# FoX attention in a hybrid trunk: diagonal probabilities masked on GpSimd, other places in SyncE's order for some transfers, query loads issued earlier

## The chip, the cores and the metric

The kernel runs on one core of one Trainium2 chip. The metric is the device time of one execution in microseconds (us), taken several times; the median is compared.

## The reference, cut to what matters

The program is one inference step of a trunk of two layers. Each layer projects the stream `x` and mixes it by three groups of heads: RWKV-7 (A), forgetting attention, called FoX (B), and gated DeltaNet (C). A gate multiplies each result, and one output projection and a LayerNorm follow. A prompt of 2048 frames and 8 running streams of 16 frames, with 1024 cached rows each, go through together. The change lies around B:

```python
def fox_attend(q, cq, qpos, k, v, ck, kpos):
    f32 = jnp.float32
    s = jnp.einsum('bqhd,bkhd->bhqk', q.astype(f32), k.astype(f32)) * (HEAD_DIM ** -0.5)
    s = s + jnp.transpose(cq, (0, 2, 1))[..., :, None] - jnp.transpose(ck, (0, 2, 1))[..., None, :]
    s = jnp.where(kpos[None, :] <= qpos[:, None], s, -jnp.inf)
    p = jax.nn.softmax(s, axis=-1)
    return jnp.einsum('bhqk,bkhd->bqhd', p, v.astype(f32))
```

`c` is the running sum of the log forget values; there are 8 heads of 64. Causality is the `where`: a key later than the query counts nothing.

## The kernel before, in words

**Stages.** Each layer goes through a projection stage, a FoX stage and an output projection. In the projection stage `proj` takes the tokens in three parts and multiplies them with groups of weight columns (`load_w` loads a raw weight `wr` and splits it into a high part `wh` and a low part `wl`; the low part is written to `wd` at its first use and loaded as `wl<-wd` later). Matmuls named `pm` and `pv` are these. Keys and queries are split into `khi` and `klo` and written to the scratch tensors KS and QS (`qs<-khi` in the profile), and the gates' inputs to PZ. The tasks of RWKV and DeltaNet run beside it, and reach into the FoX stage.

**FoX for the prompt** (`fox_prompt`). The heads go in 4 pairs, the queries in 4 blocks of 512. For a head and block `fx_max` makes scores with queries on the partitions (`mx`), and VectorE takes their row maxima (`m`); `fx_shift` turns these to two rows (`rr`, transposed by TensorE as `rrp`) and writes them into the query tile `QA`. `fx_exp` then makes the scores with 128 keys on the partitions and up to 512 queries (`st`): one matmul of `KB` and `QB`, one of `KA` and `QA` (which carry high parts, running sums and maxima), ScalarE's exponential gives `pt`. The sum of `pt` over keys (`acc`) is kept by VectorE where the key step j is a multiple of 3, and by GpSimd otherwise. `fx_pv` multiplies `pt` with the values (`fo`), two key steps of two heads at a time; these four tiles are called a **quad** here. `fx_out` divides and gates.

**The diagonal.** In the last four key steps of a block (j from 4b on) the first 128 columns of the tile hold the diagonal, and keys later than the query must go. `fx_exp` adds a third matmul there, of the constants `ngb` and `idb`, that adds a large negative number to them (`st<-idb,ngb`); `fx_max` does the same on `mx`. Per layer 4 pairs, 4 blocks, 4 steps and 2 heads make 128 of each.

**What sets the order.** A class `Model` keeps a modelled time for each tile, bank and engine while the program is written out. Every instruction goes through `Eng.__getattr__` (L246) or `PE.add` (L224; transposes, L227), so these are the lines of nearly all rows. The modelled time becomes its priority; for SyncE, whose transfers must keep one order, `Eng.order` puts each transfer by its modelled time among the ones before it, and this is fixed. `fx_pv` of a quad is put off until the modelled time at which its `pt` are ready (`self.pvt`), and other matmuls may be placed ahead of it. Transfers are issued from SyncE's queue in that order, so a transfer that waits for its data holds up all behind it.

**Opening FoX** (`open_fx`). Tiles `QA` and `KA` number 6 each; two of each exist before the stage. The other four of each are filled with constants on GpSimd (`fx_fill`), then loads of the `QA` for block 1 are issued (`fx_qa`). The cached streams (`fox_sample`) load `qx`, `kx`, `lf`, `kc` and `vc` in the same stretch. The weights of the output projection come in by `wor` near the end of the stage.

Of the kernel before, what the change touches and what calls it, by code (L numbers as in the profile page):

```python
# [14 lines left out]
TS = 16  # L15
# [89 lines left out]
class Model:  # L105
# [60 lines left out]
    def op(self, eng, kind, outs, ins):  # L166
# [13 lines left out]
        if eng == "sync":  # L180
            n = max(n * a.shape[0] for a in outs)
            cost = max(0.5, n * 4 / 3.6e5)
            end = self.place(eng, t, cost) + 2.0
            t = end - 2.0 - cost
        elif eng == "scalar" and kind == "dma_start":
            end = self.place(eng, t + 0.1, 0.45) + 2.0
            t = end - 2.45
        else:
            cost = self.cost(eng, kind, n, outs, ins)
            end = self.place(eng, t, cost)  # L190
            t = end - cost
# [107 lines left out]
class Trunk:  # L299
# [127 lines left out]
    def load_w(self, pool, key, src, kk, n, eng):  # L427
# [8 lines left out]
        if key in self.wd:  # L436
            nc.sync.dma_start(wl.bitcast(F32), self.wd[key])
        else:
            eng.tensor_tensor(wl, raw, wh.bitcast(F32), op=ALU.subtract)
            self.wd[key] = self.dram.tile([128, kk, n], F32, name="wd_" + "_".join(map(str, key)))  # L440
            nc.sync.dma_start(self.wd[key], wl.bitcast(F32))
        return wh, wl
# [93 lines left out]
    def proj(self, l, ti, groups, nxt=None):  # L536
# [91 lines left out]
        for nm, c0, S, X in (("k", 1664, self.KS[l], self.KX[l]), ("q", 1152, self.QS[l], self.QX[l])):  # L628
            if nm not in groups:
                continue  # L630
            for r in range(0, 512, 128):
# [8 lines left out]
                nc.vector.tensor_tensor(lo[:, ns:n], st[:, ns:n], hi[:, ns:n].bitcast(F32), op=ALU.subtract)  # L640
                nc.sync.dma_start(S[0, r:r + 128, tp], hi[:, ns:n].bitcast(F32))
                nc.sync.dma_start(S[1, r:r + 128, tp], lo[:, ns:n].bitcast(F32))
                if ns:
# [33 lines left out]
    def logf(self, l, ti, fs):  # L677
# [10 lines left out]
        nc.vector.scalar_tensor_tensor(out=lt, in0=f, scalar=0.0, in1=ab, op0=ALU.min, op1=ALU.subtract)  # L688
        nc.sync.dma_start(self.o["fox_logf_p"][l, 0, tp].rearrange("(j p) h -> p j h", p=128), lt[:, ns // 128:])
        if ns:  # L690
            nc.sync.dma_start(self.o["fox_logf_s"][l].rearrange("s t h -> (s t) h"), lt[:, 0])
        nc.vector.tensor_scalar(f, lt, -1.0, None, op0=ALU.mult)
        nc.sync.dma_start(self.SM[l][t0:t0 + n].rearrange("(j p) c -> p j c", p=128), fs[:, :, 8:16])
        yield
# [7 lines left out]
        if ns:  # L702
            nc.sync.dma_start(self.LX[l].rearrange("s h t -> h s t"), fr[0:8, 0:ns].rearrange("h (s t) -> h s t", t=TS))
        cr = pool.tile([8, 768], F32, tag="st", name="cr", bufs=2)
# [5 lines left out]
        self.split(ch[:, ns:n], cl[:, ns:n], cr[:, ns:n], "vector")  # L710
        nc.sync.dma_start(self.CK[l][0, :, tp], ch[:, ns:n].bitcast(F32))
        nc.sync.dma_start(self.CK[l][1, :, tp], cl[:, ns:n].bitcast(F32))

# [577 lines left out]
    def both_chain(self, x):  # L1291
# [66 lines left out]
        if x["t0"] + W == NTOK:  # L1358
            dst = self.o["gdn_wkv_p"][x["l"]].rearrange("s (p h) k v -> s p (h k) v", h=2)
            for p in range(2):  # L1360
                nc.sync.dma_start(dst[0, p], self.Sg[:, p])

# [95 lines left out]
    def gdn_chain(self, x):  # L1458
# [50 lines left out]
        for p in range(2):  # L1509
            nc.sync.dma_start(dst[:, p].rearrange("s k v -> k s v"), SS[:, :, p])  # L1510
# [39 lines left out]
    def fx_fill(self, eng, KA, QA):  # L1550
        for t in QA + KA:
            eng.memset(t[64:96].bitcast(F32), 0.0)
# [16 lines left out]
    def open_fx(self, l):  # L1569
# [98 lines left out]
    def fx_exp(self, l, pair, b):  # L1668
# [3 lines left out]
        for j in range(nk):  # L1672
# [4 lines left out]
            for hh in range(2):  # L1677
# [115 lines left out]
    def fox_sample(self, l):  # L1793
# [30 lines left out]
        for j0 in (0, 4):  # L1824
# [84 lines left out]
        z = pool.tile([128, 4, 128], F32, tag="vn", name="sfz", bufs=2)  # L1909
        nc.sync.dma_start(z, self.PZ[l][256:768, 0:SMP].rearrange("(c p) t -> p c t", p=128))  # L1910
# [4 lines left out]
        nc.sync.dma_start(self.OD[l][256:768, 0:SMP].rearrange("(c p) t -> p c t", p=128), oT)  # L1915
        self.close(pool)
# [154 lines left out]
```

## Time and profile before

| | |
|---|---|
| median of 3 runs | 4135.79 us (4131.1 to 4138.03) |
| the profiled execution, its own time | 4139.12 us |
| its span | 4137.2 us |
| mean granted TensorE clock, share of full speed | 0.95 |

The span is what the profiler saw between the first and the last instruction; the time has 1.9 us more around it. In rows, a group of instructions has its busy time, which for TensorE holds overlapped work, and the idle time of its engine just before, put down to what ended it. L224 and L246 are the lines of the helpers through which everything is issued, so groups are told apart by the names of their tiles.

### The profile page before, as it was taken

To read this page: it belongs to the slowest core of one execution; us is meant where nothing else is said; L and a number is where in the kernel's file an instruction comes from. 1 tells how busy PE (TensorE), PEld (TensorE's weight loads), DVE (VectorE), ACT (ScalarE), POOL (GpSimd) and SP (SyncE) were. 2 spreads that over 40 slices of the span, in tenths; PEclk is the share of its full clock that TensorE was granted. 3 is DMA by queue.
4 is the path that set the end of the run, shared out by engine and by line. 5 is a ranking of instruction groups with operands and counts; after the bars stand their busy time and mean duration, and the time that the engine had idled before them with its cause. 6 is when DMAs were issued, how large, how long until landed. Compare 5 with 4: busy or idle time off the path is not lost.

```text
span 4137.2 us, 78111 instructions
## 1 busy us (share of the span) xinstructions
PE 3776.2 (91%) x30554; PEld 3107.2 (75%) x30554; DVE 2700.3 (65%) x6029; ACT 1637.1 (40%) x3351; POOL 1223.7 (30%) x1073
## 2 busy tenths in 40 slices
PE   6989998999998799889999898989999888998998
PEld 6988887888887456557888888878888775665577
DVE  6475668677774677774523757577667767777645
ACT  2343434344442344542124434244435424444411
POOL 4311232122212344454222112312122124444522
PEclk9999999999998899999999999999999989999999
DMA  7744545444555677443456445554445555774332
GB/s 262 238 154 129 155 141 173 123 139 127 173 156 138 187 192 195 138 102 111 135 157 192 134 133 151 168 153 127 141 128 186 154 131 164 199 195 124 105 115 102
DMA packets 601754, 633.80 MB, mean 153 GB/s; under 512 B 153625, under 2 KB 457483, under 8 KB 601387
## 3 DMA queue, kind: packets, MB, share of 16 engines
q1 hardware_dynamic: 535228, 543.89, 45.1%
q10 hardware_dynamic: 63406, 76.01, 5.2%
q0 software_dynamic: 2752, 8.92, 0.6%
q8 instruction: 241, 3.95, 0.4%
q14 instruction: 127, 1.03, 0.1%
HBM read 437.59 MB, written 191.10 MB: 152 GB/s over the span
## 4 chain that ended last, share of the span: by engine, by line
PE 54%; DVE 19%; issue 10%; DMA 8%; POOL 4%; ACT 3%; SPq 1%; ACTq 0%; POOLq 0%; DVEq 0%
PE pm L224 21%; PE op L224 6%; PE st L224 5%; PE fo L224 4%; PE mx L224 3%; DVE itmp L246 2%; PE pv L224 2%; DVE Wi L246 2%; PE cr L224 2%; DVE y L246 2%; PE co L224 2%; DMA pc<-pc 2%; DVE xs L246 1%; DVE m L246 1%; PE cg L224 1%
## 5 line engine op out<-in xcount | busy, mean ns | idle before, releaser
L224 PE MATMUL pm<-xh,wh 128*128 128x384 f32 (+1 forms) x2784 | 987.1, 355 | 4.8 <-ACT wh L246 4.8
L224 PE MATMUL pm<-xh,wl 128*128 128x384 f32 (+1 forms) x2784 | 924.5, 332 | 23.4 <-DMA wl<-wd 14.1
L224 PE MATMUL pm<-xl,wh 128*128 128x384 f32 (+1 forms) x2784 | 923.3, 332 | 0.0
L224 PEld LDWEIGHTS pm<-xh,wh 128*128 128x128 f32 x2784 | 533.4, 192 | 43.9 <-issue 17.0
L224 PEld LDWEIGHTS pm<-xh,wl 128*128 128x128 f32 x2784 | 532.6, 191 | 27.1 <-DMA wl<-wd 16.5
L224 PEld LDWEIGHTS pm<-xl,wh 128*128 128x128 f32 x2784 | 534.0, 192 | 10.2 <-issue 9.8
L246 POOL TENSOR_TENSOR acc<-acc,pt 128x512 f32<-128x512 f32 (+2 forms) x336 | 378.3, 1142 | 347.0 <-ACT pt L246 314.0
L246 DVE TENSOR_REDUCE m<-mx 128x1 f32<-128x512 f32 (+3 forms) x640 | 371.4, 605 | 160.4 <-PE mx L224 151.6
L246 ACT ACTIVATE pt<-st 128x512 f32<-128x512 f32 (+3 forms) x640 | 330.9, 533 | 341.8 <-PE st L224 319.7
L246 ACT CAST wh<-wr 128x1024 fp32r<-128x1024 f32 (+1 forms) x198 | 207.3, 1049 | 316.8 <-PE pm L224 237.3
L224 PE MATMUL mx<-KA,QA 66*128 66x512 f32 (+3 forms) x640 | 265.1, 437 | 40.0 <-DMA QA<-qs 26.0
L224 PE MATMUL st<-QB,KB 128*128 128x512 f32 (+3 forms) x640 | 266.7, 417 | 32.1 <-DMA QB<-qs 10.7
L224 PE MATMUL fo<-pt,V 128*64 128x512 f32 (+3 forms) x1280 | 286.8, 570 | 1.1 <-ACT pt L246 1.1
L246 ACT COPY st<-pm 128x384 f32<-128x384 f32 (+1 forms) x348 | 159.2, 457 | 279.7 <-PE pm L224 265.0
L224 PE MATMUL st<-QA,KA 104*128 104x512 f32 (+3 forms) x640 | 244.0, 381 | 0.2
L246 POOL TENSOR_SCALAR SD<-Sr,dl 128x64 f32<-128x64 f32 x128 | 66.9, 537 | 594.5 <-DVE Sr L246 517.9
L224 PEld LDWEIGHTS mx<-KA,QA 66*128 66x128 f32 x640 | 128.8, 206 | 113.3 <-issue 47.0
L224 PE MATMUL op<-woh,oh 128*128 128x512 f32 x544 | 213.0, 392 | 0.7 <-ACT acc L246 0.7
L224 PE MATMUL op<-wol,oh 128*128 128x512 f32 x544 | 212.5, 391 | 0.0
L224 PE MATMUL op<-woh,ol 128*128 128x512 f32 x544 | 212.4, 390 | 0.0
L246 POOL TENSOR_TENSOR wl<-wr,wh 128x1024 fp32r<-128x1024 f32 x58 | 142.1, 2451 | 191.9 <-ACT wh L246 171.6
L246 DVE TENSOR_TENSOR itmp<-N,Wi 128x126 f32<-128x126 f32 (+22 forms) x558 | 178.7, 320 | 15.1
(378 smaller groups left out, 7616.8 us busy)
## 6 DMA issues: line engine op xcount, KB each, us to landing
wr<-in_w_in SPq DMA_DIRECT2D x198, 512.0 KB
wl<-wd SPq DMA_DIRECT2D x116, 512.0 KB
kc<-in_cache_fox_k SPq DMA_DIRECT2D x32, 1024.0 KB
vc<-in_cache_fox_v SPq DMA_DIRECT2D x32, 1024.0 KB
wd<-wl SPq DMA_DIRECT2D x58, 512.0 KB
xin<-xd SPq DMA_DIRECT2D x78, 256.0 KB
y<-xd SPq DMA_DIRECT2D x34, 512.0 KB
ol<-od SPq DMA_DIRECT2D x34, 512.0 KB
```

Source lines behind the costliest of these rows:

```text
L224: self.add(lambda: self.eng.matmul(out, a, b, start=start, stop=stop), out, a, b, cyc, start)
L246: r = f(*a, **b)
```

## The change

1. `fx_exp` no longer adds the mask matmul to `st` on the diagonal. After the exponential GpSimd sets the entries of `pt[:, :128]` to zero whose key is later than the query (`affine_select`, which goes by position and reads no mask). The mask matmul on `mx` stays.
2. A class `Lag` issues some transfers with 6 us added to their modelled time, so they take a later place in SyncE's order. These are write-outs (`wd`, `qs<-khi` and `klo`, log forget values, running sums, states, `od<-oT`) and loads of the gates' inputs `z` and of everything that `fox_sample` reads. The model now also knows that a load from a scratch tensor (name beginning with SC) comes after the write to it.
3. `open_fx` issues the loads of `QA` for block 1 ahead of the fills, and fills `QA[2:4]` first, then `KA[2:]` and `QA[4:]`.

```diff
+        self.lag = 0.0
...
             if a.space == bass.MemoryType.DRAM:
                 dram = True
+                if a.tensor.name.startswith("SC"):
+                    t = max(t, self.done.get(a.tensor.name, 0.0) - self.lag)
...
-            end = self.place(eng, t, cost) + 2.0
+            end = self.place(eng, t + self.lag, cost) + 2.0
...
+class Lag:
+    BY = 6.0
...
+    def dma_start(self, *a):
+        self.m.lag = self.BY
+        r = self.eng.dma_start(*a)
+        self.m.lag = 0.0
+        return r
...
-            nc.sync.dma_start(self.wd[key], wl.bitcast(F32))
+            nc.lag.dma_start(self.wd[key], wl.bitcast(F32))
...
-                nc.sync.dma_start(S[0, r:r + 128, tp], hi[:, ns:n].bitcast(F32))
-                nc.sync.dma_start(S[1, r:r + 128, tp], lo[:, ns:n].bitcast(F32))
+                nc.lag.dma_start(S[0, r:r + 128, tp], hi[:, ns:n].bitcast(F32))
+                nc.lag.dma_start(S[1, r:r + 128, tp], lo[:, ns:n].bitcast(F32))
...
-        nc.sync.dma_start(z, self.PZ[x["l"]][r0:r0 + 256, x["t0"]:x["t0"] + W].rearrange("(q p) t -> p q t", p=128))
+        nc.lag.dma_start(z, self.PZ[x["l"]][r0:r0 + 256, x["t0"]:x["t0"] + W].rearrange("(q p) t -> p q t", p=128))
...
-        self.fx_fill(nc.gpsimd, self.KA[2:], self.QA[2:])
         self.fx_qa(l, 0, 1)
+        self.fx_fill(nc.gpsimd, (), self.QA[2:4])
+        self.fx_fill(nc.gpsimd, self.KA[2:], self.QA[4:])
...
-                self.pe.matmul(p[:, :w], ka[0:104, ks], qa[0:104, q0:], start=False, stop=not diag)
-                if diag:
-                    self.pe.matmul(p[:, :128], self.ngb, self.idb, start=False, stop=True)
+                self.pe.matmul(p[:, :w], ka[0:104, ks], qa[0:104, q0:], start=False, stop=True)
                 pt = pool.tile([128, 512], F32, tag="pt", name="pt", bufs=8)
                 nc.scalar.activation(pt[:, :w], p[:, :w], AF.Exp, scale=0.125)
+                if diag:
+                    nc.gpsimd.affine_select(out=pt[:, :128], in_=pt[:, :128], pattern=[[1, 128]], compare_op=ALU.is_ge, fill=0.0, base=0, channel_multiplier=-1)
...
-        nc.sync.dma_start(qx, self.QX[l].rearrange("(c p) t -> p c t", p=128))
+        nc.lag.dma_start(qx, self.QX[l].rearrange("(c p) t -> p c t", p=128))
...
-                nc.sync.dma_start(t, i["cache_fox_" + nm[0]][l, s, hf * 512:hf * 512 + 512].rearrange("(j p) h d -> p j (h d)", p=128))
+                nc.lag.dma_start(t, i["cache_fox_" + nm[0]][l, s, hf * 512:hf * 512 + 512].rearrange("(j p) h d -> p j (h d)", p=128))
```

The class adds two lines, so the helpers' lines become L227, L230 and L249. What it does to the order of instructions shows at three places.

First place: TensorE in layer 1, pair 2, block 3, around the `fo` matmuls of its first diagonal quad (`st` are the scores, `idb` and `ngb` the mask). Before:

```order
L224 MATMUL st_41000<-QA5_36152,KA5_36156 128x384
L224 MATMUL st_41000<-idb_87,ngb_88 128x128
L224 MATMUL st_41007<-QB_40037,KB_39509 128x256
L224 MATMUL st_41007<-QA4_36151,KA4_36155 128x256
L224 MATMUL st_41007<-idb_87,ngb_88 128x128
L224 MATMUL st_41016<-QB_40040,KB_39514 128x256
L224 MATMUL st_41016<-QA5_36152,KA5_36156 128x256
L224 MATMUL st_41016<-idb_87,ngb_88 128x128
L224 MATMUL fo_40559<-pt_40963,V_39512 64x512
L224 MATMUL fo_40559<-pt_40978,V_39517 64x512
L224 MATMUL fo_40559<-pt_40988,V_39512 64x384
L224 MATMUL fo_40559<-pt_41004,V_39517 64x384
```

and with the change, the same quad, one row further at each end:

```order
L227 MATMUL st_41000<-QB_40040,KB_39508 128x384
L227 MATMUL st_41000<-QA5_36275,KA5_36279 128x384
L227 MATMUL st_41007<-QB_40037,KB_39503 128x256
L227 MATMUL st_41007<-QA4_36274,KA4_36278 128x256
L227 MATMUL st_41016<-QB_40040,KB_39508 128x256
L227 MATMUL st_41016<-QA5_36275,KA5_36279 128x256
L227 MATMUL fo_40616<-pt_40962,V_39506 64x512
L227 MATMUL fo_40616<-pt_40977,V_39511 64x512
L227 MATMUL fo_40616<-pt_40987,V_39506 64x384
L227 MATMUL fo_40616<-pt_41003,V_39511 64x384
L227 MATMUL st_41027<-QB_40037,KB_39503 128x128
```

The three mask matmuls are gone, and nothing has come between the last scores and `fo`. On POOL (GpSimd) the selects of this quad's four `pt` now stand so, with the adds of the sums `acc` between:

```order
L249 AFFINE_SELECT pt_40962<-pt_40962 128x128
L249 AFFINE_SELECT pt_40977<-pt_40977 128x128
L249 AFFINE_SELECT pt_40987<-pt_40987 128x128
L249 TENSOR_TENSOR acc_40505<-acc_40505,pt_40987 128x384
L249 AFFINE_SELECT pt_41003<-pt_41003 128x128
L249 TENSOR_TENSOR acc_40506<-acc_40506,pt_41003 128x384
```

The select of the fourth `pt` (`pt_41003`) has come to stand behind an add.

Second place: SyncE's transfers as FoX opens in layer 0, behind the last weight loads `wl` (`QA2` and `QA3` are the query tiles for block 1). Before:

```order
L246 DMA wl_14779<-wd_0_3080_5575 128x1024
L246 DMA z_15026<-pz0_108 128x2x256
L246 DMA out_gdn_wkv_p<-Sg_14846 128x64 x2
L246 DMA QB_14940<-qs0_114 64x512
L246 DMA QB_14943<-qs0_114 64x512
L246 DMA KB_14946<-ks0_112 64x1024
L246 DMA V_14949<-vs0_124 128x8x64
L246 DMA QB_14940<-qs0_114 64x512
L246 DMA QB_14943<-qs0_114 64x512
L246 DMA KB_14946<-ks0_112 64x1024
L246 DMA KB_14951<-ks0_112 64x1024
L246 DMA QA2_14914<-qs0_114 64x512
```

and with the change:

```order
L249 DMA wl_14735<-wd_0_3080_5575 128x1024
L249 DMA QA2_14845<-qs0_114 64x512
L249 DMA QA3_14846<-qs0_114 64x512
L249 DMA QB_14871<-qs0_114 64x512
L249 DMA QB_14874<-qs0_114 64x512
L249 DMA KB_14877<-ks0_112 64x1024
L249 DMA V_14880<-vs0_124 128x8x64
L249 DMA QB_14871<-qs0_114 64x512
L249 DMA QB_14874<-qs0_114 64x512
L249 DMA KB_14877<-ks0_112 64x1024
```

`QA2` and `QA3` have moved ahead of all `QB`, `KB` and `V`, and the gate's `z` and the state's write-out `out_gdn_wkv_p` have moved behind.

Third place: the same queue, some transfers later (`QB_15161` before and `QB_15108` after are the queries for block 1; `qx`, `kx`, `lf`, `kc`, `vc` and `vn` belong to the cached streams). Before:

```order
L246 DMA z_15034<-pz0_108 128x2x256
L246 DMA qx_15064<-qx0_120 128x4x128
L246 DMA kx_15065<-kx0_118 128x4x128
L246 DMA lf_15072<-in_cache_fox_logf 128x8x64
L246 DMA kc_15077<-in_cache_fox_k 128x4x512
L246 DMA KA2_14918<-ck0_116 2x1024
L246 DMA KA3_14919<-ck0_116 2x1024
L246 DMA QA5_14917<-qs0_114 64x512
L246 DMA vn_15248<-vs0_124 16x512
L246 DMA kc_15103<-in_cache_fox_k 128x4x512
L246 DMA vc_15122<-in_cache_fox_v 128x4x512
L246 DMA KB_15151<-ks0_112 64x1024
```

and with the change:

```order
L249 DMA KB_15098<-ks0_112 64x1024
L249 DMA V_15101<-vs0_124 128x8x64
L249 DMA KB_15103<-ks0_112 64x1024
L249 DMA QB_15108<-qs0_114 64x512
L249 DMA KB_15098<-ks0_112 64x1024
L249 DMA V_15106<-vs0_124 128x8x64
L249 DMA KB_15103<-ks0_112 64x1024
L249 DMA QB_15108<-qs0_114 64x512
L249 DMA QB_15111<-qs0_114 64x512 x2
L249 DMA z_15132<-pz0_108 128x2x256
L249 DMA qx_15148<-qx0_120 128x4x128
L249 DMA kx_15149<-kx0_118 128x4x128
```

The keys, values and queries have moved ahead of `z`, `qx`, `kx`, `lf` and `kc`.

## Rows read from the trace of the kernel before

**Rows 1.** the page's busy times of the engines and instruction counts

```profile
PE 3776.2 (91%) x30554; PEld 3107.2 (75%) x30554; DVE 2700.3 (65%) x6029; ACT 1637.1 (40%) x3351; POOL 1223.7 (30%) x1073
```

**Rows 2.** windows: us; PE PEld DVE ACT POOL busy; clock, DMA share, GB/s

```profile
1320.00:1400.00 80.00, 53.17 (x207) 35.28 (x208) 48.21 (x99) 23.16 (x42) 32.15 (x35) 0.70 0.75 180
1400.00:1897.00 497.00, 458.54 (x2881) 275.38 (x2877) 354.79 (x631) 235.79 (x442) 238.73 (x202) 0.95 0.54 148
3358.00:3450.00 92.00, 76.98 (x485) 51.81 (x484) 58.68 (x131) 26.03 (x50) 35.15 (x41) 0.71 0.61 150
3450.00:3935.00 485.00, 445.70 (x2838) 268.39 (x2838) 346.69 (x622) 234.96 (x437) 228.92 (x197) 0.96 0.56 154
```

**Rows 3.** groups by form (busy us, mean ns), the mask matmul on the scores

```profile
L224 PE MATMUL st<-idb,ngb 128*128 128x128 f32 x256 | 62.4, 244 | 0.0
```

**Rows 4.** timeline of TensorE (start, us, what), a diagonal quad in layer 1

```profile
3815.05 0.22 PE L224 MATMUL st<-idb,ngb 128*128 128x128 f32 x1
3815.11 0.33 PE L224 MATMUL st<-QB,KB 128*128 128x256 f32 x1
3815.90 1.72 PE L224 MATMUL fo<-pt,V 128*64 128x512 f32 x8
```

**Rows 5.** groups by form on POOL (busy us, mean ns, idle before)

```profile
L246 POOL TENSOR_TENSOR acc<-acc,pt 128x128 f32<-128x128 f32 x32 | 16.1, 507 | 44.0 <-ACT pt L246 40.3 <-DVE sfm L246 2.7 <-issue 1.0
L246 POOL TENSOR_TENSOR acc<-acc,pt 128x384 f32<-128x384 f32 x32 | 32.7, 1035 | 30.9 <-ACT pt L246 29.4 <-DVE acc L246 1.4
L246 POOL TENSOR_SCALAR SD<-Sr,dl 128x64 f32<-128x64 f32 x128 | 66.9, 537 | 594.5 <-DVE Sr L246 517.9 <-DVE dl L246 55.5 <-DVE itmp L246 21.0
```

**Rows 6.** timelines of ScalarE, POOL and VectorE at the same quad

```profile
3815.31 1.15 ACT L246 ACTIVATE pt<-st 128x384 f32<-128x384 f32 x3 [0.35 <-PE st L224]
...
3815.04 3.51 POOL L246 TENSOR_TENSOR acc<-acc,pt 128x384 f32<-128x384 f32 x4 [2.54 <-ACT pt L246]
...
3816.18 1.01 DVE L246 TENSOR_SCALAR rr<-m 128x4 fp32r<-128x4 f32 x1
```

**Rows 7.** the tile rr (ns min/median/max), and who waited for it (us, times)

```profile
L246 DVE TENSOR_SCALAR rr<-m x64: 150/258/1726, 1324.8 to 3903.1; 128x4 fp32r<-128x4 f32 x64
L246 DVE SCALAR_TENSOR_TENSOR rr<-m,rr x64: 145/164/1237, 1329.1 to 3903.6; 128x4 fp32r<-128x4 f32 x64
...
  PE rrp L227: 32.2, 28
```

**Rows 8.** timelines of TensorE, SyncE's queue and POOL, FoX start, layer 0

```profile
1334.16 0.76 PE L224 MATMUL mx<-KA,QA 66*128 66x512 f32 x1 [7.66 <-DMA QA<-qs]
...
1321.92 1.09 SPq L246 DMA_DIRECT2D QB<-qs  x2
1328.97 1.18 SPq L246 DMA_DIRECT2D QA<-qs  x2
...
1327.63 1.92 POOL L246 MEMSET QA<- 2x512 f32 x4
```

**Rows 9.** the same, somewhat later: TensorE and SyncE's queue

```profile
1377.35 0.79 PE L224 MATMUL st<-QB,KB 128*128 128x512 f32 x1 [10.66 <-DMA QB<-qs]
...
1348.15 1.07 SPq L246 DMA_DIRECT2D kc<-in_cache_fox_k  x1
1368.67 1.23 SPq L246 DMA_DIRECT2D QB<-qs  x2
```

**Rows 10.** waits of TensorE (us in total, times, longest us)

```profile
PE mx L224 <- DMA QA<-qs: 26.0, 6, 11.4
PE pt L227 <- DMA xin<-xd: 24.8, 11, 4.5
PE pm L224 <- DMA wl<-wd: 14.1, 7, 4.9
```

**Rows 11.** timeline of SyncE's queue, layer 1

```profile
3812.89 9.62 SPq L246 DMA_DIRECT2D wor<-in_w_out  x8
```

More of the change, by code (lines that the diff above doesn't have):

```diff
@@ L265, in order, with __init__ @@
             del ls[:100]
+class Lag:
+    BY = 6.0
+    def __init__(self, eng, model):
+        self.eng, self.m = eng, model
+    def dma_start(self, *a):
[3 more added lines that the diff above has]
+        return r
 class NC:
@@ L272, in __init__ @@
             setattr(self, n, Eng(n, getattr(nc, n), model))
+        self.lag = Lag(self.sync, model)
 class Pool:
@@ L688, in logf @@
         nc.vector.scalar_tensor_tensor(out=lt, in0=f, scalar=0.0, in1=ab, op0=ALU.min, op1=ALU.subtract)
-        nc.sync.dma_start(self.o["fox_logf_p"][l, 0, tp].rearrange("(j p) h -> p j h", p=128), lt[:, ns // 128:])
+        nc.lag.dma_start(self.o["fox_logf_p"][l, 0, tp].rearrange("(j p) h -> p j h", p=128), lt[:, ns // 128:])
         if ns:
-            nc.sync.dma_start(self.o["fox_logf_s"][l].rearrange("s t h -> (s t) h"), lt[:, 0])
+            nc.lag.dma_start(self.o["fox_logf_s"][l].rearrange("s t h -> (s t) h"), lt[:, 0])
         nc.vector.tensor_scalar(f, lt, -1.0, None, op0=ALU.mult)
-        nc.sync.dma_start(self.SM[l][t0:t0 + n].rearrange("(j p) c -> p j c", p=128), fs[:, :, 8:16])
+        nc.lag.dma_start(self.SM[l][t0:t0 + n].rearrange("(j p) c -> p j c", p=128), fs[:, :, 8:16])
         yield
@@ L702, in logf @@
         if ns:
-            nc.sync.dma_start(self.LX[l].rearrange("s h t -> h s t"), fr[0:8, 0:ns].rearrange("h (s t) -> h s t", t=TS))
+            nc.lag.dma_start(self.LX[l].rearrange("s h t -> h s t"), fr[0:8, 0:ns].rearrange("h (s t) -> h s t", t=TS))
         cr = pool.tile([8, 768], F32, tag="st", name="cr", bufs=2)
@@ L710, in logf @@
         self.split(ch[:, ns:n], cl[:, ns:n], cr[:, ns:n], "vector")
-        nc.sync.dma_start(self.CK[l][0, :, tp], ch[:, ns:n].bitcast(F32))
-        nc.sync.dma_start(self.CK[l][1, :, tp], cl[:, ns:n].bitcast(F32))
+        nc.lag.dma_start(self.CK[l][0, :, tp], ch[:, ns:n].bitcast(F32))
+        nc.lag.dma_start(self.CK[l][1, :, tp], cl[:, ns:n].bitcast(F32))
     def open_rg(self, l):
@@ L1360, in both_chain @@
             for p in range(2):
-                nc.sync.dma_start(dst[0, p], self.Sg[:, p])
+                nc.lag.dma_start(dst[0, p], self.Sg[:, p])
     def rwkv_chain(self, x):
@@ L1509, in gdn_chain @@
         for p in range(2):
-            nc.sync.dma_start(dst[:, p].rearrange("s k v -> k s v"), SS[:, :, p])
+            nc.lag.dma_start(dst[:, p].rearrange("s k v -> k s v"), SS[:, :, p])
     def gate(self, x, r0, y, name):
@@ L1550, in fx_fill @@
     def fx_fill(self, eng, KA, QA):
-        for t in QA + KA:
+        for t in (*QA, *KA):
             eng.memset(t[64:96].bitcast(F32), 0.0)
@@ L1797, in fox_sample @@
         kx = pool.tile([128, 4, 128], F32, name="kx")
-        nc.sync.dma_start(qx, self.QX[l].rearrange("(c p) t -> p c t", p=128))
-        nc.sync.dma_start(kx, self.KX[l].rearrange("(c p) t -> p c t", p=128))
+        nc.lag.dma_start(qx, self.QX[l].rearrange("(c p) t -> p c t", p=128))
+        nc.lag.dma_start(kx, self.KX[l].rearrange("(c p) t -> p c t", p=128))
         qbd = pool.tile([128, NS, 4, 32], F32, name="qbd")
@@ L1805, in fox_sample @@
         lf = pool.tile([128, NS, 8, 8], F32, tag="vn", name="lf", bufs=2)
-        nc.sync.dma_start(lf, i["cache_fox_logf"][l].rearrange("s (p j) h -> p s j h", j=8))
+        nc.lag.dma_start(lf, i["cache_fox_logf"][l].rearrange("s (p j) h -> p s j h", j=8))
         lr = pool.tile([64, PAST + TS], F32, tag="S", name="lr64", bufs=2)
@@ L1828, in fox_sample @@
             nc.scalar.mul(lv[:, j0:j0 + 4], p[0:64].rearrange("p (j t) -> p j t", j=4), -1.0)
-        nc.sync.dma_start(lr[:, PAST:], self.LX[l].rearrange("s h t -> (s h) t"))
+        nc.lag.dma_start(lr[:, PAST:], self.LX[l].rearrange("s h t -> (s h) t"))
         cr = pool.tile([64, PAST + TS], F32, tag="S", name="cr64", bufs=2)
@@ L1909, in fox_sample @@
         z = pool.tile([128, 4, 128], F32, tag="vn", name="sfz", bufs=2)
-        nc.sync.dma_start(z, self.PZ[l][256:768, 0:SMP].rearrange("(c p) t -> p c t", p=128))
+        nc.lag.dma_start(z, self.PZ[l][256:768, 0:SMP].rearrange("(c p) t -> p c t", p=128))
         g = pool.tile([128, 4, 128], F32, tag="vn", name="sfg", bufs=2)
@@ L1914, in fox_sample @@
         nc.vector.tensor_tensor(oT, oT, g, op=ALU.mult)
-        nc.sync.dma_start(self.OD[l][256:768, 0:SMP].rearrange("(c p) t -> p c t", p=128), oT)
+        nc.lag.dma_start(self.OD[l][256:768, 0:SMP].rearrange("(c p) t -> p c t", p=128), oT)
         self.close(pool)
```

## Prediction

> **What bounds the kernel now.** I read the busy times of the engines first. TensorE is busy for 91% of the span, GpSimd (POOL) for 30% [rows 1]. Next the stretches: the two FoX stages proper (1400 to 1897 us and 3450 to 3935 us) hold TensorE busy for 458.54 of 497 us and 445.70 of 485 us, both 92%, and POOL for 238.73 and 228.92 us, some 48% [rows 2]. So a TensorE instruction taken out of a FoX stage is worth nearly its issue time, and POOL has room, if what it is given is not waited for. The reader should then see the two short stretches ahead of them (1320 to 1400 and 3358 to 3450 us): only 53.17 of 80 us and 76.98 of 92 us are busy, at a mean granted clock of 0.70 and 0.71 [rows 2]. There the kernel waits for transfers. Of TensorE's waits by what ended them, three belong to SyncE's queue and to this change: 26.0 us for `QA`, 24.8 us for `xin` and 14.1 us for `wl` [rows 10]. The sum is made against the profiled execution, 4139.1 us, which is 3.3 us above the median of the runs (4135.8).
>
> **A. 256 mask matmuls leave TensorE.** They show 62.4 us of busy time [rows 3], but that is overlapped: the mask matmul that starts at 3815.05 is followed by the next matmul at 3815.11, so one takes 0.06 us of the queue [rows 4]. 256 x 0.06 = 15.4 us, of which 92% counts where TensorE is the bound: **14 us won**. From below it is 0 (the slot is left empty because something else is late, which is term B); from above 15.4. By the Trainium skill ("TensorE: Matmul & The Clock Gate", section "Back-to-back issue gap") a weight load and its matmul of 128 columns take about 81 ns in a sustained stream, by which the term would be 20.7 us; the row says 0.06 us, and the row decides.
>
> **B. 256 selects arrive on POOL, between the exponential and the product with V.** No row has a select. The nearest are two-input adds of the same 128x128 shape, 507 ns, and `SD`, which has one tensor as input and 64 columns, 537 ns [rows 5]. I take 0.5 us; the ends are 0.1 us (a fixed part alone) and 1.07 us (twice `SD`, if it went by columns). 256 x 0.5 = 128 us of POOL, 64 us for each layer: its share of a FoX stage rises from 48% to 61%, so throughput is not the limit. The delay is. Take the quad that `fo` finishes from 3815.90 on [rows 4]. Its last exponential is the first of the three that start at 3815.31 and take 1.15 us together [rows 6]; the other two are the next quad's. It ends at about 3815.8, 0.1 us ahead of `fo`. With the change the fourth `pt` of the quad waits for its select too, and in POOL's order an add of 128x384 (1.04 us, [rows 5]) stands directly ahead of that select. Add and select are 1.5 us; 0.1 us of slack and the three `fo` matmuls that go first (eight take 1.72 us, so 0.6, [rows 4]) cover 0.7; the quad is 0.8 us late. There are 64 diagonal quads (2 layers x 4 pairs x 4 blocks x 2). In the order of the changed kernel 16 of them, the first quads of blocks 2 and 3, have no more matmuls between their last score and `fo` than before (first place in the section on the change); in the other 48 other matmuls have moved in between. So 16 x 0.8 = **13 us lost**; the ends are 0 (all covered) and 64 x 1.4 = 90 us (every quad, with the select at 1.07 us).
>
> **C. A busier POOL holds up VectorE.** `rr`, on 128x4, takes from 150 ns to 1.73 us, and 145 ns to 1.24 us in its second form [rows 7]; the one at 3816.18 takes 1.01 us while POOL adds from 3815.04 to 3818.55 [rows 6]. TensorE waits for `rr` 28 times, 32.2 us in all [rows 7]. If such waits grow as POOL's share does, 61 to 48, that is 32.2 x 0.27 = **9 us lost**; ends 0 and 32.2 (doubled).
>
> **D. Early queries.** At the start of FoX in layer 0 TensorE waits 7.66 us for `QA` [rows 8]. SyncE issued that load only at 1328.97, behind eight others from 1321.92 on, and POOL had finished filling the four `QA` only at 1329.55, since the `KA` were filled between [rows 8]. In the changed order the two `QA` loads stand first, ahead of all `QB` and `KB`, and their fill is half as long and comes first (second place). I take **8 us won**: most of these 7.66, and something of the four shorter waits in the row's total (26.0 less 7.7 and 11.4 leaves 6.9, [rows 10]). Ends 0 (what waited for `QA` waits for `KB` behind it) and 10.
>
> **E. Unhurried loads.** At 1377.35 TensorE has waited 10.66 us for `QB` [rows 9]. The load for block 1 went out at 1368.67, twenty microseconds after `kc` at 1348.15 [rows 9], a load of cached keys that these scores do not need; `z`, `qx`, `kx` and `lf` went with it. In the changed order `KB`, `V` and `QB` stand ahead of them all (third place): **8 us won**, ends 0 and 10.7.
>
> **F. The clock.** In both short stretches some 130 us of matmuls ran at a mean granted clock of 0.70 [rows 2]. With the two long idle times gone the mean may rise; to 0.74 it gives 130 x (1 - 0.70/0.74) = 7 us. I take **6 us won**, ends 0 and 16 (0.80).
>
> **G. The `wor` loads.** In layer 1 eight loads of the output weights hold SyncE for 9.62 us [rows 11], and `QA` behind them is TensorE's longest wait, 11.4 us [rows 10]. In the changed order both layers have `wor` in two fours with `KA` loads between. One long stall becomes shorter in one layer and one appears in the other: **0**, ends -10 (5 us, half of 9.62, in each layer on top) and +11.
>
> **H. Projection stages.** Loads of `wl` and `xin` stand in SyncE's order behind write-outs of `khi` and `klo`, which cannot go before VectorE has made them. With 6 us more in their modelled time they go later. 14.1 us wait on `wl`, 24.8 us on `xin` [rows 10]; I take **10 us won**, a quarter. From above 39 us, if all goes; from below -24: write-outs that leave later free the three buffers of their ring later, at four places (keys and queries in each layer) by up to the 6 us that the class adds.
>
> **Nothing.** The later `od`, `logf` and state write-outs cost nothing beside: they are read only a stage later, and if that cover goes, the reader (`ol` in the output projection) waits at most the 6 us once a layer.
>
> **Sum.** 14 - 13 - 9 + 8 + 8 + 6 + 0 + 10 = 24 us won; 4139.1 - 24 = 4115, and less 3.3 to stand against the median, **4112 us**.
>
> **The rivals.**
> 1. *The queue was the larger part.* H is 39 and C is 0: 38 us more, 4074 us. For it: the waits are there [rows 10]. Against: nothing in the change moves a load of `xin` itself. Chance 0.12.
> 2. *The stalls only move.* D and E are given back because the loads that now stand later (`kc`, `KA`, `wor`) are late in their turn: 4112 + 16 = 4128 us. For it: eight `wor` still hold SyncE 9.62 us [rows 11]. Chance 0.10.
> 3. *VectorE is held up.* C is 32.2 in place of 9: 4112 + 23 = 4135 us, no change. For it: `rr` is computed beside the diagonal quads, where the selects are [rows 6]. Against: selects are short beside the adds of 1.04 us [rows 5]. The Trainium skill ("SBUF — State Buffer", section "Who interferes with whom") has this as a rule: VectorE and GpSimd share a pair of ports, and one of them holds it for a whole instruction while the other is blocked. The spread of `rr` in rows 7 agrees, as does the 1.01 us above. Chance 0.09.
> 4. *POOL's queue is the new wait* (slower). The select stands behind adds in every quad, not in 16, and takes 1.07 us: B is 90 in place of 13, 4112 + 77 = 4189 us. It decides from 0.70 us a quad on: 64 x 0.70 = 45, which is 32 more than 13 and brings 4144. For it: slack of 0.1 us in the quad read, and POOL's adds alternate with selects. Against: in 48 quads matmuls moved in between. Chance 0.17.
>
> That the change does not do what it says is excluded by the order: the 256 matmuls are gone from TensorE's, the selects stand in POOL's.
>
> **How the numbers follow.** My forecast has the rest, 0.52, with a range of its own from 4095 to 4127. A measurement of this kernel can tell about 0.2%, 8.3 us. Forecast and rival 1 are faster by more: 0.64. Rivals 2 and 3 are within it: 0.19. Rival 4: 0.17. The range goes from 4075 (the mild half of rival 1) to 4152 (rivals 2 and 3 whole and the mild part of 4), leaving out the rest of these two, some 0.19.
>
> **What would show it.** In the profile after: the group of mask matmuls on `st` gone and `mx`'s still there; a select of some 0.5 us on POOL, 256 times, POOL at about 1350 us. Waits of TensorE's `fo` for POOL `pt` of 13 us in all (B); above 45 us rival 4 holds. PE `rrp` waiting for `rr` some 41 us (C). The waits for `QA` at 1334 and `QB` at 1377 below 2 us (D, E), and the clock of the two short stretches at 0.74 or more (F). `wl` and `xin` waits together below 30 us (H). The forecast is wrong if TensorE's busy share in FoX falls below 92% by more than the 14 us that leave it, or if the select takes over 0.9 us.

## The result, and the profile after

The changed kernel takes 4171.35 us (median of 4, 4168.93 to 4185.18), the kernel before 4135.84 us (4131.1 to 4138.03): a ratio of 1.0089, with an interval from 1.0069 to 1.0108. It is **slower by about 36 us**. The forecast was 4112 us, and the range ended at 4152. Two executions, one of the kernel before (4587.62 us) and one of an experiment (selects aside, 4669.18 us), ran at a granted clock of 0.74 and 0.72 in place of 0.95 and are left out of what is compared.

The stretches of [rows 2], in the profile after (4168.93 us, span 4167.0 us; columns as there):

```profile
1320.00:1400.00 80.00, 58.00 (x332) 35.46 (x331) 51.70 (x115) 25.62 (x49) 37.79 (x53) 0.83 0.77 178
1400.00:1897.00 497.00, 439.56 (x2684) 256.53 (x2682) 346.11 (x618) 226.40 (x427) 258.89 (x296) 0.93 0.53 149
3358.00:3450.00 92.00, 73.49 (x469) 51.17 (x466) 55.82 (x122) 25.07 (x50) 38.77 (x56) 0.78 0.66 158
3450.00:3935.00 485.00, 428.03 (x2632) 251.88 (x2628) 343.29 (x616) 216.39 (x407) 244.26 (x285) 0.92 0.54 152
```

The openings of FoX went as forecast: more work in 1320 to 1400, clock 0.83 and 0.78 in place of 0.70 and 0.71. The loss is in the two long stretches. TensorE's share there falls from 92% to 88%, by 19 and 18 us of busy time, and the clock from 0.95 and 0.96 to 0.93 and 0.92. The prediction had named a fall by more than the 14 us that leave TensorE as a sign that it is wrong. The tile `fo` shows the length of the stage: the first line is layer 0 and the second layer 1, with first and last start at the end of the times.

```profile
L227 PE MATMUL fo<-pt,V x640: 272/593/1117, 1356.0 to 1910.4; 128*64 128x512 f32 x112, 128*64 128x384 f32 x16, 128*64 128x256 f32 x16, 128*64 128x128 f32 x16
L227 PE MATMUL fo<-pt,V x640: 272/592/1117, 3411.7 to 3969.3; 128*64 128x512 f32 x112, 128*64 128x384 f32 x16, 128*64 128x256 f32 x16, 128*64 128x128 f32 x16
```

That is 554.4 and 557.6 us. Before, the same two views give 1361.9 to 1892.7 and 3401.3 to 3935.6, 530.8 and 534.3 us. Each layer loses some 23 us between its first and its last product with V, and outside of these the kernel takes about 17 us less.

The selects themselves are cheap (group on POOL, columns as in [rows 5]):

```profile
L249 POOL TENSOR_SCALAR_AFFINE_SELECT pt<-pt 128x128 f32<-128x128 f32 x256 | 86.1, 347 | 155.5 <-ACT pt L249 150.3 <-DVE S L249 2.7 <-DMA V<-vs 1.1
```

0.35 us each, not the 0.5 that was taken. What grew are TensorE's waits; these are FoX's for VectorE and POOL (us in all, times, longest):

```profile
PE rrp L230 <- DVE rr L249: 49.0, 30, 2.8
...
PE st L227 <- DVE m L249: 14.2, 14, 2.4
...
PE fo L227 <- DVE fu L249: 11.0, 8, 3.7
PE mx L227 <- DVE QA L249: 10.9, 4, 3.1
PE mx L227 <- DVE m L249: 9.9, 11, 4.0
...
PE st L227 <- DVE QA L249: 8.1, 6, 2.8
PE fo L227 <- POOL pt L249: 8.0, 8, 1.8
...
PE rrp L230 <- DVE m L249: 4.7, 1, 4.7
```

Only 8.0 us are waits of `fo` for a select. The rest of the list is VectorE, 107.8 us. The same waits before, of FoX's five kinds of matmul (`rrp`, `mx`, `st`, `fo` and `lp`) for VectorE, sum to 63.0 us; the wait on `rr` among them was 32.2 us [rows 7]. And VectorE itself waits for POOL (its waits for the sums `acc`):

```profile
DVE acc L249 <- POOL pt L249: 69.4, 50, 5.1
...
DVE acc L249 <- POOL acc L249: 27.5, 12, 4.9
```

96.9 us; before it was 38.3 us, all of it for POOL's `acc`. The last diagonal steps of block 3, in the first pair of layer 0, show how it goes (timelines of ScalarE, POOL, VectorE and TensorE, in this order):

```profile
1485.02 1.38 ACT L249 ACTIVATE pt<-st 128x384 f32<-128x384 f32 x5 [0.21 <-PE st L227]
...
1485.25 1.00 POOL L249 TENSOR_TENSOR acc<-acc,pt 128x384 f32<-128x384 f32 x1
1486.21 0.29 POOL L249 TENSOR_SCALAR_AFFINE_SELECT pt<-pt 128x128 f32<-128x128 f32 x1
1486.59 0.99 POOL L249 TENSOR_TENSOR acc<-acc,pt 128x384 f32<-128x384 f32 x1
1487.54 0.53 POOL L249 TENSOR_SCALAR_AFFINE_SELECT pt<-pt 128x128 f32<-128x128 f32 x2
1488.04 1.40 POOL L249 TENSOR_TENSOR acc<-acc,pt 128x256 f32<-128x256 f32 x2
1489.40 0.53 POOL L249 TENSOR_SCALAR_AFFINE_SELECT pt<-pt 128x128 f32<-128x128 f32 x2
...
1486.58 0.15 DVE L249 TENSOR_REDUCE m<-m 128x4 f32<-128x8 f32 x1
...
1489.72 0.35 DVE L249 TENSOR_TENSOR acc<-acc,pt 128x128 f32<-128x128 f32 x1 [2.87 <-POOL pt L249]
1490.00 0.15 DVE L249 TENSOR_SCALAR rr<-m 128x4 fp32r<-128x4 f32 x1
...
1490.47 0.27 PE L230 MATMUL rrp<-cst,rr 128*8 128x128 f32 x1 [2.81 <-DVE rr L249]
```

Key step 15 is a multiple of 3, so its sum is VectorE's. Its exponential is done by 1486.40, but its selects (the two at 1489.40) stand behind POOL's adds for key steps 13 and 14 (1.00, 0.99 and 1.40 us). VectorE stands still for 2.87 us at the add that needs the first of them. The row maxima `m` had been ready since 1486.73, but `rr` is queued behind that add, and TensorE waits 2.81 us for `rr`. Counted by key step in the trace, VectorE's sums wait 23.0 us for POOL at key step 15, 18.9 us at key step 12 of block 3 and 8.3 us at key step 3 of block 0.

At the start of a pair the selects stand behind other work too, the gate products `ft` of the pair before (layer 1, first block of the last pair, key step 3; POOL, then VectorE):

```profile
3865.49 1.26 POOL L249 TENSOR_TENSOR ft<-fu,ft 128x512 f32<-128x512 f32 x1
...
3867.97 0.81 DVE L249 TENSOR_TENSOR acc<-acc,pt 128x128 f32<-128x128 f32 x1 [2.63 <-POOL pt L249]
```

### The profile page after: what moved, and what is told of

It is laid out like the page before. It is cut to its first block, busy times and chain, and to the rows that moved or that the text cites. A ratio compares the mean times of both kernels' runs of the same rounds, so it can differ in the third digit from the quotient of the medians.

```text
span 4167.0 us, 77720 instructions
## 1 busy us (share of the span) xinstructions
PE 3773.3 (91%) x30298; PEld 3086.9 (74%) x30298; DVE 2703.6 (65%) x6029; ACT 1622.3 (39%) x3351; POOL 1310.5 (31%) x1329
## 4 chain that ended last, share of the span: by engine, by line
PE 53%; DVE 19%; issue 9%; POOL 7%; DMA 6%; ACT 4%; SPq 1%; ACTq 0%; POOLq 0%; DVEq 0%
PE pm L227 22%; PE op L227 6%; PE fo L227 4%; PE st L227 4%; DVE Wi L249 2%; DVE itmp L249 2%; PE pv L227 2%; PE mx L227 2%; POOL acc L249 2%; DVE y L249 2%; PE cr L227 2%; PE co L227 1%; DVE m L249 1%; DVE acc L249 1%; DMA pc<-pc 1%
## 5 line engine op out<-in xcount | busy, mean ns | idle before, releaser
L227 PE MATMUL pm<-xh,wh 128*128 128x384 f32 (+1 forms) x2784 | 989.8, 356 | 5.4 <-ACT wh L249 3.6
L227 PE MATMUL pm<-xh,wl 128*128 128x384 f32 (+1 forms) x2784 | 925.2, 332 | 24.4 <-POOL wl L249 16.0
L227 PE MATMUL pm<-xl,wh 128*128 128x384 f32 (+1 forms) x2784 | 924.2, 332 | 0.0
L227 PEld LDWEIGHTS pm<-xh,wh 128*128 128x128 f32 x2784 | 534.0, 192 | 45.2 <-issue 17.7
L227 PEld LDWEIGHTS pm<-xh,wl 128*128 128x128 f32 x2784 | 532.7, 191 | 28.0 <-POOL wl L249 18.4
L227 PEld LDWEIGHTS pm<-xl,wh 128*128 128x128 f32 x2784 | 534.6, 192 | 11.0 <-issue 10.6
L249 ACT ACTIVATE pt<-st 128x512 f32<-128x512 f32 (+3 forms) x640 | 326.2, 533 | 343.8 <-PE st L227 318.2
L249 POOL TENSOR_TENSOR acc<-acc,pt 128x512 f32<-128x512 f32 (+2 forms) x336 | 377.9, 1136 | 255.0 <-ACT pt L249 205.6
L249 DVE TENSOR_REDUCE m<-mx 128x1 f32<-128x512 f32 (+3 forms) x640 | 368.5, 604 | 137.5 <-PE mx L227 134.5
L249 ACT CAST wh<-wr 128x1024 fp32r<-128x1024 f32 (+1 forms) x198 | 207.7, 1049 | 314.2 <-PE pm L227 263.5
L227 PE MATMUL fo<-pt,V 128*64 128x512 f32 (+3 forms) x1280 | 308.8, 600 | 19.0 <-DVE fu L249 11.0
L227 PE MATMUL st<-QB,KB 128*128 128x512 f32 (+3 forms) x640 | 268.4, 422 | 32.8 <-DVE m L249 14.2
L227 PE MATMUL mx<-KA,QA 66*128 66x512 f32 (+3 forms) x640 | 257.5, 424 | 30.5 <-DVE QA L249 10.9
L249 ACT COPY st<-pm 128x384 f32<-128x384 f32 (+1 forms) x348 | 158.7, 456 | 276.5 <-PE pm L227 259.2
L227 PE MATMUL st<-QA,KA 104*128 104x512 f32 (+3 forms) x640 | 242.9, 383 | 1.1 <-DVE QA L249 1.1
L249 POOL TENSOR_SCALAR SD<-Sr,dl 128x64 f32<-128x64 f32 x128 | 65.9, 528 | 559.5 <-DVE Sr L249 444.8
L227 PE MATMUL op<-woh,oh 128*128 128x512 f32 x544 | 212.0, 390 | 1.4 <-ACT acc L249 1.4
L227 PE MATMUL op<-wol,oh 128*128 128x512 f32 x544 | 211.8, 389 | 0.0
L227 PE MATMUL op<-woh,ol 128*128 128x512 f32 x544 | 211.8, 389 | 0.0
L249 DVE TENSOR_TENSOR acc<-acc,pt 128x512 f32<-128x512 f32 (+3 forms) x176 | 135.7, 781 | 115.4 <-POOL pt L249 63.0
L227 PEld LDWEIGHTS fo<-pt,V 128*64 128x64 f32 x1280 | 89.0, 150 | 160.8 <-issue 119.0
L249 POOL TENSOR_TENSOR wl<-wr,wh 128x1024 fp32r<-128x1024 f32 x58 | 144.7, 2497 | 192.0 <-ACT wh L249 186.3
```

The lines of the kernel that those rows point to most:

```text
L227: self.add(lambda: self.eng.matmul(out, a, b, start=start, stop=stop), out, a, b, cyc, start)
L249: r = f(*a, **b)
```

## The experiments

Ratios are against runs of the kernel before on the same chip, with the interval in brackets. The changed kernel was not run again beside the experiments, so differences in us against it are between medians of several chips. The kernel before took 4135.84 us beside it and some 4139 to 4141 beside the experiments; by the ratios these differences would be 2 to 5 us larger.

**1. Which part costs, and is it the wait or POOL's time?** The selects alone, put into the kernel before:

```diff
-                self.pe.matmul(p[:, :w], ka[0:104, ks], qa[0:104, q0:], start=False, stop=not diag)
-                if diag:
-                    self.pe.matmul(p[:, :128], self.ngb, self.idb, start=False, stop=True)
+                self.pe.matmul(p[:, :w], ka[0:104, ks], qa[0:104, q0:], start=False, stop=True)
...
+                if diag:
+                    nc.gpsimd.affine_select(out=pt[:, :128], in_=pt[:, :128], ...)
```

> The kernel before with the selects in place of the mask matmuls and nothing else of the change. Theory W (VectorE's and TensorE's queues wait behind instructions that need a select): the loss is here and the transfers gave something back, so this is slower than the whole change, about 4171 + 21 = 4192 us. Theory L (POOL's added time blocks VectorE, whoever needs the select): the same, 4192 us. Theory T (the new places of the transfers cost the time): 4122 to 4136 us, no slower than before.

4176.45 us, 1.0096 (1.0077 to 1.0116). The selects alone cost 38 us and more than the whole change. T falls; W and L had the direction, and 16 us too much.

The other way round, the changed kernel with the `+` and `-` of this diff exchanged:

> The changed kernel with the mask matmuls put back and no select: later transfers and early queries alone. W and L: FoX in layer 0 begins some 14 us earlier, in layer 1 some 7 us, and nothing is lost in it: about 4136 - 21 = 4115 us. T: the loss stays and 14 us of matmuls come on top, 4171 + 14 = 4185 us.

4125.35 us, 0.997 (0.9955 to 0.9985). Later transfers and early queries win some 13 us. That is 46 us less than the changed kernel takes, though 256 matmuls more are in it. FoX's waits of TensorE were 107.8 us for VectorE and 8.0 for POOL; here they are 69.5 (the rows below and three of 0.6 us or less) and none:

```profile
PE rrp L230 <- DVE rr L249: 41.5, 30, 4.1
...
PE rrp L230 <- DVE m L249: 7.9, 2, 5.7
...
PE mx L227 <- DVE m L249: 6.0, 13, 1.0
PE lp L227 <- DVE acc L249: 5.2, 2, 2.8
PE st L227 <- DVE QA L249: 5.0, 8, 0.8
...
PE st L227 <- DVE m L249: 2.4, 7, 0.5
```

Then the selects on POOL beside the mask matmuls, with nobody waiting for them:

```diff
+                    jk = pool.tile([128, 128], F32, tag="jk", name="jk", bufs=2)
+                    nc.gpsimd.affine_select(out=jk, in_=pt[:, :128], ...)
```

> The mask matmuls do the masking, and the 256 selects run on POOL too, into a tile that nobody reads. POOL carries the same added time, but no instruction of another engine needs it. W: within 10 us of the run without selects, 4115 to 4125 us. L: VectorE is held up as in the changed kernel, about 4171 + 14 = 4185 us.

4127.87 us, 0.9981 (0.9967 to 0.9994), some 3 to 5 us above the run without selects, with intervals that overlap. POOL carries the same load, as its group by form shows:

```profile
L249 POOL TENSOR_SCALAR_AFFINE_SELECT jk<-pt 128x128 f32<-128x128 f32 x256 | 91.5, 363 | 183.3 <-ACT pt L249 147.6 <-DMA KB<-ks 33.2 <-DMA V<-vs 1.1
```

and in TensorE's waits of this run the one for `rr` is no longer than before the change (32.2 us):

```profile
PE rrp L230 <- DVE rr L249: 30.1, 23, 3.3
```

So L falls as the main cause and W stands: the cost comes with the wait for the select's result.

The same without selects and without mask matmuls:

> The changed kernel with neither select nor mask matmul on the scores of the second pass: it leaves out the causal mask of the probabilities in the diagonal tiles. It prices what the 256 matmuls are worth where nothing takes their place: against the run with the matmuls and no selects 14 us less by the prediction's term A, 4101 us under W and L.

4108.03 us, 0.9932 (0.9912 to 0.9952): 17 us below the run with the matmuls. That is the worth of the 256 matmuls; what the changed kernel pays for doing without them is 4171 - 4108 = 63 us. It is paid in the FoX stages. From the first to the last `fo` of each layer, in the changed kernel and then in this run (columns as in [rows 2]):

```profile
1356.00:1910.40 554.40, 483.77 (x2865) 280.61 (x2865) 376.00 (x670) 246.10 (x466) 291.74 (x340) 0.92 0.53 149
3411.70:3969.30 557.60, 488.85 (x2864) 284.59 (x2864) 376.94 (x670) 246.28 (x466) 292.66 (x340) 0.92 0.53 148
...
1357.40:1878.50 521.10, 469.79 (x2870) 274.10 (x2869) 382.91 (x673) 249.74 (x471) 251.32 (x216) 0.95 0.56 158
3380.50:3905.90 525.40, 475.41 (x2870) 277.55 (x2869) 381.00 (x673) 249.88 (x471) 251.32 (x215) 0.93 0.56 157
```

With nearly the same matmuls the two stages are 65.5 us longer: TensorE stands idle for 38 us more, and is busy for 27 us more, at a granted clock of 0.92 in place of 0.95 and 0.93. So some two fifths of the loss are not waits but slower matmuls. Whether it is the waits that bring the clock down was not tested.

**2. Who must not wait?** The division of the sums between VectorE and POOL is one line:

```diff
-                    eng = nc.vector if j % 3 == 0 else nc.gpsimd
+                    eng = nc.vector if j % 3 == 0 and not diag else nc.gpsimd
```

> The changed kernel, but the sums of the diagonal tiles are all added on POOL, so that no VectorE instruction waits for a select. Theory V (VectorE stands in order behind adds that wait for a select, and the maxima and rr behind them come late): most of the loss of some 50 us goes, less what a busier POOL costs; about 4135 us. Theory F (TensorE's own fo matmuls wait for the selects, in POOL's queue): POOL's queue only gets longer, 4171 to 4190 us.

4125.63 us, 0.9971 (0.9954 to 0.9988): 46 us below the changed kernel. In the profile (of the longest of its ten executions, 4143.66 us) `fo` waits longer for selects (12.1 us in place of 8.0), and TensorE's waits for `rr` fall from 49.0 to 24.8 us. V, and by 9 us more than it had.

```diff
-                    eng = nc.vector if j % 3 == 0 else nc.gpsimd
+                    eng = nc.vector if j % 3 == 0 or diag else nc.gpsimd
```

> The changed kernel, but the sums of the diagonal tiles are all added on VectorE, so that no add of a diagonal tile stands ahead of a select in POOL's queue. V: more VectorE instructions wait for selects: 4171 to 4190 us. F: the selects come some 0.7 us sooner and fo waits less: about 4145 us.

**4113.58 us, 0.9938 (0.9918 to 0.9958)**: better still, where V expected no gain and F 31 us less of it. VectorE needs more selects, but those of the last key steps come soon, since no add of a diagonal tile stands ahead of them on POOL. The group of VectorE's adds of 128x128 shows it, in the changed kernel

```profile
L249 DVE TENSOR_TENSOR acc<-acc,pt 128x128 f32<-128x128 f32 x32 | 11.9, 380 | 31.3 <-POOL pt L249 31.3
```

and in this one (twice as many; the last part is the idle time ahead of them and what ended it):

```profile
L249 DVE TENSOR_TENSOR acc<-acc,pt 128x128 f32<-128x128 f32 x64 | 19.0, 316 | 4.1 <-POOL pt L249 4.0
```

and so do TensorE's waits of this run:

```profile
PE rrp L230 <- DVE rr L249: 23.1, 23, 3.2
...
PE fo L227 <- POOL pt L249: 3.3, 2, 1.7
```

All of VectorE's waits for POOL in its sums are still 78.3 us here, against 96.9: it matters more which add waits, and what stands behind it, than the total. Neither V nor F alone says it: the loss needs both, late selects and a VectorE that waits for them. Take either away and 46 to 58 us come back. The same sums with the mask matmuls in place of selects:

> Mask matmuls back, no selects, later transfers and early queries kept, and the diagonal sums all on VectorE. Theory Q (VectorE's sums help only because they take adds out from between the selects): no gain over the same kernel with the old sums, 4125 to 4135 us. Theory S (that division of the sums is better by itself, and the selects cost as much as before): some 40 us less, about 4085 us.

4121.19 us, 0.9954 (0.9939 to 0.9969), which cannot be told from 4125 (0.997, 0.9955 to 0.9985). Nearest to Q, and far from S: the division helps because of the selects. Giving VectorE less of the other sums (`j % 4 == 0 or diag`):

> The changed kernel with all diagonal sums on VectorE, which gives up some of its other sums in return (every fourth key step in place of every third). If VectorE's load still counts: 5 us less than with diagonal sums on VectorE alone, about 4108 us. If POOL's queue counts more: 4115 to 4125 us.

4124.9 us, 0.9962 (0.9947 to 0.9976): no help, as the second branch had it. VectorE's waits for POOL in its sums are 110.9 us here, more than in the changed kernel, which takes 46 us longer; so that total does not tell the time.

**3. Can a better order hide it?** The model adds 1.5 or 3.0 us to when a select's result is ready (`if kind == "affine_select": end += 1.5`).

> The changed kernel, where the model that sets the order takes a select's result to be ready 1.5 us later, so that fo matmuls and adds that need it are placed further back and others go ahead. V and F both: some half of the 46 to 63 us by which the selects are dearer than no selects comes back, about 4145 us. If POOL's time itself is what costs (neither V nor F): no change, 4171 us.

> The same with 3.0 us. V and F: near the kernel without selects less the matmuls, 4115 to 4135 us, unless tiles that live longer (8 buffers of pt, 4 of acc) become the new wait, then 4150 us.

4172.68 us, 1.008 (1.0052 to 1.0108), and 4164.43 us, 1.0062 (1.0038 to 1.0086). A miss. The first time is the one that the text on record gives to POOL's time itself as the cause, and the selects aside speak against that. The instructions move, but VectorE still waits 96.2 and 89.5 us for POOL in its sums, and TensorE's waits change hands: they are 379.4 us in all in the changed kernel, 378.3 and 386.2 here (`fo` for `fu`, 11.0 us in the changed kernel, is 18.4 us with 3.0 us of room). Why room does not help was not found out.

**4. Where?** Only the sum of key step 15 moved to POOL (`j % 3 == 0 and j != 15`). The text on record calls it 32 adds; it is 16 (2 layers, 4 pairs, 2 heads), since the other 16 adds of that size are key step 3's.

> The changed kernel with 32 adds of 128x128 moved: the sum of key step 15, the last of block 3, on POOL in place of VectorE. Theory H (the loss is made where VectorE's last sum of block 3 waits for a select that stands behind POOL's adds, with the maxima's rr behind it): half of the 46 to 58 us comes back, 4140 to 4150 us. Theory A (the loss is spread over all diagonal quads): under 10 us, 4161 to 4175 us.

4139.37 us, 0.9999 (0.9985 to 1.0012): **16 adds give 32 us back**.

> The changed kernel with the sums of key steps 13 and 14 on VectorE as well, so that in block 3 all diagonal sums are there, and blocks 0 to 2 are as in the change. H: half or more of the 58 us that all diagonal sums on VectorE gave, 4130 to 4142 us. A: a quarter (one block of four), 4157 us.

4142.7 us, 1.0008 (0.9994 to 1.0022): 29 us. Both are at or a little past H's expectation and far from A's. TensorE's waits with key step 15 moved:

```profile
PE rrp L230 <- DVE rr L249: 36.3, 25, 2.6
...
PE fo L227 <- POOL pt L249: 7.4, 7, 1.8
PE fo L227 <- DVE fu L249: 3.5, 6, 1.1
```

`fo` waits for selects as in the changed kernel (7.4 against 8.0 us); 12.7 us went from `rr` and 7.5 us from `fu`. The wait of `rrp` that was 2.81 us at 1490.47 is 0.24 us here. So about half of the loss is made at the end of block 3, where the last sum and the maxima for the next blocks meet on VectorE.

**5. The transfers.** Early queries alone:

> The kernel before with the early query loads and the fills in the new order, nothing else. If the prediction's term D holds: 8 us less than before, about 4130 us. If the wait only moves to the loads behind it: no change, 4134 to 4140 us.

**4114.97 us, 0.9944 (0.9925 to 0.9962)**: 23 us, three times term D, and as good as anything here. In 1310 to 1420 us the waits for `QA` (7.7) and `QB` (10.7) are both gone, against two new ones in TensorE's waits of this run:

```profile
PE mx L224 <- DMA KA<-ck: 9.4, 1, 9.4
PE rrp L227 <- DMA kx<-kx: 4.1, 1, 4.1
```

That is 5 us net, and the first `fo` starts only 1.7 us sooner. The gain is in the stage behind it: from the first to the last `fo` of layer 0 it is 507.7 us in place of 530.8, with a granted clock of 0.96 in place of 0.94, while in layer 1 it is 9 us longer. Where the rest comes from is not shown.

Later transfers alone:

> The kernel before with the later transfers alone (class Lag and the model's knowledge of the scratch tensors). If terms E and H hold: 4136 - 18 = 4118 us. If H is nothing, as the two projection stages of the changed kernel's trace suggest (they take as long as before): about 4130 us.

4138.62 us, 1.0003 (0.9986 to 1.002): nothing, and neither branch. `xin` and `wl` are better off, and the queries worse; these waits of TensorE in this run answer to [rows 10]:

```profile
PE mx L227 <- DMA QA<-qs: 46.2, 6, 14.0
PE pt L230 <- DMA xin<-xd: 15.9, 11, 3.1
PE pm L227 <- DMA wl<-wd: 7.5, 4, 2.4
```

The version without later transfers that should have been best:

> The kernel before with three things: early queries, the selects, and all diagonal sums on VectorE; transfers keep their old places. If the parts add up: 4115 (early queries alone) less the 12 us by which selects with VectorE's sums beat the matmuls under later transfers (4125 to 4113), about 4103 us.

4133.49 us, 0.999 (0.9973 to 1.0007): the parts do not add up. A stall on a transfer is back, which neither early queries alone (1.6 us) nor the whole change has (TensorE's waits of this run):

```profile
PE st L224 <- DMA QB<-qs: 19.4, 3, 17.9
```

Every edit makes a new order, and a stall of 10 to 18 us can come or go with it. So differences of that size between these kernels are not the worth of the edit alone. The 29 and 32 us of part 4 are above them, but not by much; that two edits agree there is what supports them. Why `QB` is late in this order was not tried.

## Why the prediction was wrong

- **A held.** 14 us forecast, 17 measured, between the kernels without selects with and without the matmuls. The row gave 15.4 us. By the Trainium skill ("TensorE: Matmul & The Clock Gate", section "Back-to-back issue gap"), whose 81 ns hold for a sustained stream of 128 columns, the estimate was 20.7 us. The measured 17 lies between and, with its interval, does not tell the two apart.
- **B was about right for what it named, and named too little.** It forecast 13 us of `fo` waiting for selects; 8.0 us were measured. Its price of 0.5 us was too high (0.35). But the step took `fo` for the only reader of a select. The sums `acc` read the masked `pt` too, and those of key steps 3, 6, 9, 12 and 15 are VectorE's, and in block 0 that of key step 1, which is VectorE's too although the rule in the section on the kernel before gives it to GpSimd. These readers were put at nothing, without a reason.
- **C is the step that failed.** "A busier POOL holds up VectorE" was its whole account of VectorE: held up by POOL being busy, for 9 us. Selects aside make POOL as busy and cost 3 to 5 us, within the intervals. In its place the runs showed that VectorE's adds wait for selects in order, with maxima, `rr` and `fu` queued behind: FoX's waits of TensorE for VectorE are 107.8 us with selects and 69.5 without, and moving the 16 adds of key step 15 off VectorE gives 32 us back. B asked what stands ahead of a select in POOL's queue; what stands behind the add that needs it was not asked for VectorE.
- **D and E.** Right in kind: the 7.66 and 10.66 us of [rows 8, 9] are gone in the profile after. The sizes were put to the wrong edits: early queries alone take both away and give 23 us, most of it not at these two places; later transfers, to which E gave 8 us, give none alone.
- **F held at the openings.** 0.83 and 0.78 are past the 0.74 taken. But in the long stretches the clock fell by 0.02 and 0.04, which no term had.
- **H was wrong.** The waits on `xin` and `wl` fell from 38.9 to 21.2 us, as it said they might, but other waits grew: for POOL's `wl` to 16.0 us (9.3 before), for VectorE's `wl` to 12.4 (5.3), for `TT` to 39.2 (18.3). With later transfers alone the same waits are 14.3, 13.7 and 38.5 us, and there is no gain.
- **The rivals.** 4 (POOL's queue is the new wait, 0.17) was nearest in sign and cause: selects do stand behind POOL's other work, gate products among it that B had left out. But its price assumed `fo` waiting in every quad, and its own sign, more than 45 us of `fo` waiting for POOL, did not come (8.0); that 4171 lies between its 4144 and 4189 is luck. 3 (VectorE held up) had the right engine, and its mechanism, the shared ports, is ruled out as the main cause by the selects aside.

## What to carry to other kernels

When an operation is moved off the busiest engine into the middle of a chain, list every reader of its result, and for each reader's engine what is queued behind it; the price is made there, not by the operation's length (0.35 us a piece, 63 us in all here). If the result has to come from another engine, keep its other readers from alternating between that engine and a third: sums all on either engine gave 46 to 58 us back. And try each part of a mixed change alone: an earlier place for a few loads (early queries) was worth 23 us alone and 13 us together with the later transfers, and was buried under the selects.

Of the versions that keep the mask, two are fastest and cannot be told from one another: the kernel before with early queries alone (4114.97 us) and the whole change with the diagonal sums on VectorE (4113.58 us).

## What the runs showed of the hardware

A select of 128x128 takes 0.29 us in most places (the median of 256). The one below shows 1.27 us while VectorE subtracts two tensors of 128x1024 (timelines of POOL and VectorE, changed kernel):

```profile
3842.30 1.27 POOL L249 TENSOR_SCALAR_AFFINE_SELECT pt<-pt 128x128 f32<-128x128 f32 x1
...
3841.56 3.09 DVE L249 TENSOR_TENSOR wol<-wor,woh 128x1024 fp32r<-128x1024 f32 x2
```

The select ends at 3843.57, just behind the first of the two subtractions (to 3843.42). So it looks as if the blocking that the prediction read from `rr` goes the other way as well. The Trainium skill ("SBUF — State Buffer", section "Who interferes with whom") says that a VectorE instruction with two inputs in SBUF contends with a GpSimd instruction that reads it, and this row agrees. Over the whole kernel it weighs little, as the selects aside show.
